# Seven products instead of eight for weight pair 3 in the output projection, with five raw slots and another planner table

## The chip, the cores and the metric

The kernel runs on one core of one Trainium2 chip. The metric is the device time of one execution, in microseconds (us). The core's engines each run their own instruction stream: TensorE (PE, with its weight loads shown apart as PEld), VectorE (DVE), ScalarE (ACT), GpSimd (POOL) and SyncE (SP). SP and POOL mainly start DMA transfers here. The order of the instructions on each engine is fixed when the kernel is built; at run time an instruction waits only for the semaphores that its inputs and buffers need.

## The reference

Two layers of a hybrid encoder over 256 tokens of width 4096, all in float32. Cut to what matters:

```python
for l in range(2):
    h = rmsnorm(x, norm_w[l])
    proj = h @ w_in[l]                       # (256, 4096) x (4096, 11264)
    aq, ak, av, ag, rq, rk, rv, rg = split(proj)
    a_out = silu(ag) * gqa_attention(rope(rmsnorm(aq)), rope(rmsnorm(ak)), av)
    r_out = silu(rg) * rmsnorm(bidirectional_retention(rope(rq), rope(rk), rv))
    x = x + concat(a_out, r_out) @ w_out[l]  # (256, 4096) x (4096, 4096)
return rmsnorm(x, final_norm)
```

Nearly all arithmetic is in the two projections, and they read 500 MB of weights once.

## The kernel before

**Three matmuls a product.** A float32 product is made of three matmuls in a faster format. A weight tile is split into a high part `whi` (a cast on ACT) and the rest `wlo` (a subtraction on DVE); the activations are split the same way into `x8h`, `x8l` (or `x7h`, `x7l`). PE does high times high and high times low (line 1683) and then low times high (line 1693).

**Blocks, pairs, pages.** The weights are worked off in 30 blocks of 1024 output columns: 11 of `w_in` and 4 of `w_out` in each layer. In a block the 4096 rows are taken as 16 pairs of 128-row tiles. With the two column halves and the two token halves a pair is a 2x2 by 2x2 block product: **eight** products, from two pages of 128x1024 weights, or **seven** by a Strassen-like scheme. `SEVENS` lists, for each of the four stages (w_in and w_out of layer 0, then of layer 1), the pairs that take seven: 2, 5, 8, 9, 11 and 13 everywhere. The products add up in PSUM banks M1 to M8, which `combine` folds into the two result pages `ca` and `cb` at a block's end, while PE is already in the next block.

**What a seven costs beside PE.** It needs sums of weight quarters. The first two quarters are loaded (`wraw`, 512 KB), copied by ACT to `wv`, and POOL starts a DMA that adds a second tensor from memory onto `wv` (line 729; `twice_in` or `twice_out`, 512 KB). DVE makes two more sums in `wu` from `wraw`, `wv` and the third quarter (`third`, 256 KB, line 552). So a seven gives four pages to split: `wraw` and `wv` and `wu` (128x1024 each) and `third` (128x512, parts `bhi` and `blo`). The activations of a seven need sums too: four in `xf` (128x128 each), then a split into `x7h`, `x7l`.

**Slots and the loads.** Raw pages land in `RAWS` = 6 slots, `wraw0` to `wraw5`. SP issues the load of the next page when a slot comes free (line 531): for an eight when DVE has made its `wlo`, for a seven when DVE has read it for `wu`. The loads follow the order of use, but the first page of a seven may be moved `A_EARLY` places forward in it:

```python
for i, g in enumerate(self.raws):
    if g.seven and i > RAWS + A_EARLY:
        self.raws.insert(i - A_EARLY, self.raws.pop(i))
```

With `A_EARLY` = 0 nothing is moved. High parts have a ring of five pages (`RING`), low parts of four.

**What sets the order.** A planner inside the kernel keeps a model of the time on PE, DVE and ACT while it writes the program, and puts the attention, the retention, the splitting of activations and the combining between the weight pages. The numbers in capitals (`RUSH`, `ADD_AHEAD`, `STEP_V`, `RELIEF`, ...) steer it; `PLANS` gives other values of some of them for single blocks (blocks 0 to 14 are layer 0, 15 to 29 layer 1). `SPREAD` to `SPREAD3` set where in the first block of each stage the sevens stand among the eights. In those four **opening blocks** the activations of the next stage have to be split while the last work of the stage before is still going on. All DVE and ACT instructions are recorded by one helper and so carry its line, 321.

## Time and profile before

| | us |
|---|---|
| median of 3 runs (2598.05 to 2601.19) | 2599.41 |
| the profiled execution | 2599.34 |
| its span, from the first to the last instruction | 2597.6 |

The profile is of one execution. A row of its page 5 gives a group of instructions: line, engine, operation, output and inputs, shape and count; then the busy time in us and the mean of one in ns; then how long the engine stood idle just before them and what ended that. The blocks lie one behind the other at some 83 us each; `w_out` of layer 0 opens at about 957 us, layer 1 at about 1290 us, and its `w_out` at about 2250 us.

### The profile page before, as it was taken

The numbers are of one execution on the slowest core, as the hardware profiler recorded it, in microseconds if no ns is written. First come the engines' busy times: TensorE is split into PE (matmuls) and PEld (weight loads), VectorE is DVE, ScalarE is ACT, GpSimd is POOL, SyncE is SP. The second block draws the span as 40 slices with busy tenths as digits, with TensorE's granted clock in tenths as the row PEclk, the third lists the DMA queues.
The fourth block names the chain that finished last, engine by engine and source line by source line (L and its number), as shares of the span: only waits on it lengthen the run. The fifth ranks groups of instructions, "written<-read, shape, count | busy, mean of one in ns | idle before, by whom it ended". The sixth has DMA issues, their size and how long they took to land.

```text
span 2597.6 us, 34368 instructions
## 1 busy us (share of the span) xinstructions
PE 2581.8 (99%) x11560; PEld 2135.2 (82%) x11560; DVE 2215.3 (85%) x2710; ACT 1853.6 (71%) x2626; POOL 398.6 (15%) x548
## 2 busy tenths in 40 slices
PE   9999999999999999999999999999999999999998
PEld 7888888888888888888878888888888888888886
DVE  7898888888789898777979888889888798987777
ACT  8877777766666788656887667776666667886655
POOL 0111221221102100211111112221201021000000
PEclk9999999999999999999999999999999999999999
DMA  9988988888778778988888879888887787788886
GB/s 314 305 237 277 289 242 254 281 247 263 221 220 260 230 235 227 271 269 248 275 253 261 250 239 279 246 270 268 259 257 222 208 259 242 220 229 251 250 243 194
DMA packets 206594, 653.52 MB, mean 252 GB/s; under 512 B 24784, under 2 KB 31440, under 8 KB 206416
## 3 DMA queue, kind: packets, MB, share of 16 engines
q1 hardware_dynamic: 147040, 472.99, 51.8%
q0 software_dynamic: 58656, 177.24, 30.7%
q8 instruction: 90, 1.47, 0.2%
q10 hardware_dynamic: 720, 1.10, 0.1%
q14 instruction: 88, 0.72, 0.1%
HBM read 607.19 MB, written 44.04 MB: 251 GB/s over the span
## 4 chain that ended last, share of the span: by engine, by line
PE 94%; DMA 2%; DVE 2%; ACT 1%; issue 1%; SPq 0%; DVEq 0%; POOLq 0%; POOL 0%; ACTq 0%
PE M L1683 60%; PE M L1693 30%; PE M L1158 1%; PE M L1157 1%; PE M L1156 1%; DMA ca<-in_x 1%; DVE wlo L321 1%; ACT whi L321 1%; DMA third<-in_w_out 0%; PE M L1677 0%; DMA wraw<-in_w_out 0%; DVE cb L321 0%; DMA whole<-in_w_in 0%; ACT ca L321 0%; DVE ca L321 0%
## 5 line engine op out<-in xcount | busy, mean ns | idle before, releaser
L321 DVE TENSOR_TENSOR wlo<-wraw,whi 128x1024 fp32r<-128x1024 f32 (+1 forms) x774 | 935.3, 1215 | 172.8 <-issue 61.2
L321 ACT CAST whi<-wraw 128x1024 fp32r<-128x1024 f32 (+1 forms) x776 | 800.1, 1045 | 297.1 <-PE M L1683 283.0
L1683 PE MATMUL M<-whi,x8h 128*128 128x512 f32 x2368 | 922.5, 390 | 1.0 <-DVE cb L321 0.8
L1683 PE MATMUL M<-whi,x8l 128*128 128x512 f32 x2368 | 921.8, 389 | 0.0
L1693 PE MATMUL M<-wlo,x8h 128*128 128x512 f32 x2364 | 676.3, 389 | 0.2 <-DVE wlo L321 0.2
L1683 PEld LDWEIGHTS M<-whi,x8h 128*128 128x128 f32 x2368 | 444.6, 188 | 94.9 <-DVE cb L321 1.5
L1683 PEld LDWEIGHTS M<-whi,x8l 128*128 128x128 f32 x2368 | 444.6, 188 | 92.4 <-DVE x8l L321 0.3
L1693 PEld LDWEIGHTS M<-wlo,x8h 128*128 128x128 f32 x2364 | 442.2, 188 | 91.4 <-DVE wlo L321 1.0
L1683 PE MATMUL M<-whi,x7h 128*128 128x512 f32 x1080 | 420.5, 389 | 0.2 <-ACT whi L321 0.2
L1683 PE MATMUL M<-whi,x7l 128*128 128x512 f32 x1080 | 420.3, 389 | 0.0
L1693 PE MATMUL M<-wlo,x7h 128*128 128x512 f32 x1080 | 334.4, 390 | 0.7 <-DVE wlo L321 0.6
L729 POOL DMA_DIRECT2D wv<-in_twice_in x132 | 118.5, 898 | 1068.6 <-ACT wv L321 923.8
L321 ACT CAST whi<-wu 128x1024 fp32r<-128x1024 f32 x180 | 189.3, 1052 | 91.9 <-DVE wu L321 54.2
L321 ACT CAST whi<-wv 128x1024 fp32r<-128x1024 f32 x180 | 189.0, 1050 | 91.5 <-PE M L1683 51.9
L321 DVE TENSOR_TENSOR wlo<-wv,whi 128x1024 fp32r<-128x1024 f32 x180 | 219.6, 1220 | 37.3 <-PE M L1693 30.7
L321 ACT COPY wv<-wraw 128x1024 f32<-128x1024 f32 x180 | 188.9, 1049 | 74.7 <-DMA wraw<-in_w_out 35.2
L321 DVE TENSOR_TENSOR wlo<-wu,whi 128x1024 fp32r<-128x1024 f32 x180 | 219.1, 1217 | 24.8 <-PE M L1693 16.7
L1693 PEld LDWEIGHTS M<-wlo,x7h 128*128 128x128 f32 x1080 | 202.4, 188 | 44.1 <-DVE wlo L321 2.5
L1683 PEld LDWEIGHTS M<-whi,x7h 128*128 128x128 f32 x1080 | 202.8, 188 | 42.6 <-ACT whi L321 0.9
L1683 PEld LDWEIGHTS M<-whi,x7l 128*128 128x128 f32 x1080 | 202.8, 188 | 41.8
L321 DVE TENSOR_TENSOR wu<-wu,third 128x512 f32<-128x512 f32 x180 | 124.6, 692 | 7.0 <-DMA third<-in_w_in 0.8
L321 DVE TENSOR_TENSOR wu<-wraw,wv 128x512 f32<-128x512 f32 x180 | 123.1, 684 | 8.7 <-DMA wv<-in_twice_in 6.3
(249 smaller groups left out, 2292.0 us busy)
## 6 DMA issues: line engine op xcount, KB each, us to landing
wraw<-in_w_in SPq DMA_DIRECT2D x568, 512.0 KB, 5.2
wraw<-in_w_out SPq DMA_DIRECT2D x208, 512.0 KB, 5.4
wv<-in_twice_in POOLq DMA_DIRECT2D x132, 512.0 KB, 7.5
third<-in_w_in SPq DMA_DIRECT2D x132, 256.0 KB, 5.8
wv<-in_twice_out POOLq DMA_DIRECT2D x48, 512.0 KB, 8.1
third<-in_w_out SPq DMA_DIRECT2D x48, 256.0 KB, 5.7
full<-next_dram POOLq DMA_DIRECT2D x18, 512.0 KB, 9.5
p_dram<-room POOLq DMA_DIRECT2D x64, 128.0 KB, 3.4
```

Source lines behind the costliest of these rows:

```text
L321: return call(out, *args, **kwargs)
L729: self.adds.pop(0)[1]()
L1156: nc.tensor.matmul(out, a[0], b[0], start=start, stop=False)
L1157: nc.tensor.matmul(out, a[0], b[1], start=False, stop=False)
L1158: nc.tensor.matmul(out, a[1], b[0], start=False, stop=stop)
L1683: nc.tensor.matmul(acc[name], a[i], g.hi[h], start=m == first[name] and not i, stop=False)
L1693: nc.tensor.matmul(acc[name], a, g.lo[h], start=False, stop=m == final[name])
```

## The change

Pair 3 takes seven products in stages 1 and 3, the eight `w_out` blocks; in `w_in` it stays an eight. `EVER`, the pairs that are a seven anywhere, grows from six to seven, and with it the `x7h` and `x7l` pages. The raw slots go from six to five, and `A_EARLY` from 0 to 1. The positions in the opening blocks and the planner's table are others, so nearly every row of every engine's order has another neighbour. Over the whole program PE has 11542 instructions in place of 11566: each of the eight blocks loses one product of three matmuls. DVE has 2752 in place of 2712, ACT 2436 in place of 2409; POOL gains eight DMA starts onto `wv`, and SP eight of `third` and eight fewer of `wraw`.

```diff
-RAWS = 6
-A_EARLY = 0
+RAWS = 5
+A_EARLY = 1
...
-RUSH = 1.0
+RUSH = 2.0
...
-ADD_AHEAD = 1.0
+ADD_AHEAD = 3.0
...
 PLANS = {
-    1: {'LOW_AHEAD': 5.0},
-    6: {'TIGHT_A': 8},
...
+    0: {'STEP_V': 3.0, 'BANK_REST': 0.5, 'LOW_AHEAD': 1.0, 'RELIEF': 1.0, 'AT_ONCE': 3},
+    1: {'STEP_V': 2.5, 'QUEUE': 1.0},
...
-SEVENS = ((2, 5, 8, 9, 11, 13), (2, 5, 8, 9, 11, 13), (2, 5, 8, 9, 11, 13), (2, 5, 8, 9, 11, 13))
+SEVENS = ((2, 5, 8, 9, 11, 13), (2, 3, 5, 8, 9, 11, 13), (2, 5, 8, 9, 11, 13), (2, 3, 5, 8, 9, 11, 13))
...
-SPREAD = (3, 5, 8, 11, 12, 13)
-SPREAD1 = (4, 7, 8, 10, 12, 14)
-SPREAD2 = (2, 3, 6, 7, 10, 13)
-SPREAD3 = (6, 7, 9, 11, 12, 14)
+SPREAD = (4, 5, 7, 11, 12, 13)
+SPREAD1 = (4, 6, 7, 10, 11, 12, 15)
+SPREAD2 = (2, 3, 6, 7, 12, 13)
+SPREAD3 = (3, 6, 7, 9, 11, 12, 13)
```

Three places in the order, all of layer 0. **Place A** is on DVE where the last `w_in` block ends and the first `w_out` block begins: the combining of the finished block (`cb`, `ca` from the banks M), and behind it the low part of the first weight page of `w_out` that is needed next (`wlo_8773` before, `wlo_8805` in the change; the numbers only tell buffers apart). Before:

```order
L321 TENSOR_TENSOR wlo_8727<-wraw1_8533,whi_8708 128x1024
L321 TENSOR_TENSOR x7l_8697<-xf_8698,x7h_8696 128x640
L321 TENSOR_TENSOR cb_8644<-ca_8643,M6_8244 128x512
L321 TENSOR_TENSOR ca_8643<-cb_8644,M7_8150 128x512
L321 SCALAR_TENSOR_TENSOR cb_8644<-ca_8643,M5_8147 128x512
L321 SCALAR_TENSOR_TENSOR cb_8644<-cb_8644,M5_8147 128x512
L321 TENSOR_TENSOR cb_8644<-cb_8644,out_8757 128x512
L321 TENSOR_TENSOR cb_8644<-cb_8644,M8_7952 128x512
L321 TENSOR_TENSOR wlo_8773<-wraw2_8591,whi_8722 128x1024
```

The same place on DVE in the change:

```order
L327 TENSOR_TENSOR wlo_8756<-wraw0_8616,whi_8732 128x1024
L327 TENSOR_TENSOR cb_8669<-ca_8668,M6_8249 128x512
L327 TENSOR_TENSOR ca_8668<-cb_8669,M7_8144 128x512
L327 SCALAR_TENSOR_TENSOR cb_8669<-ca_8668,M5_8139 128x512
L327 SCALAR_TENSOR_TENSOR cb_8669<-cb_8669,M5_8139 128x512
L327 TENSOR_TENSOR cb_8669<-cb_8669,out_8773 128x512
L327 TENSOR_TENSOR cb_8669<-cb_8669,out_8785 128x512
L327 TENSOR_TENSOR ca_8668<-ca_8668,M4_7967 128x512
L327 TENSOR_TENSOR ca_8668<-ca_8668,M2_7971 128x512
L327 TENSOR_TENSOR wlo_8805<-wraw3_8634,whi_8740 128x1024
```

The two sums onto `ca` now stand ahead of the low part, and the second sum onto `cb` reads a copy that ACT made (`out`) instead of bank M8; the `x7l` that stood here has moved up.

**Place B** is on ACT some 60 us earlier, in the last `w_in` block: sixteen small copies that move a result page (`ca<-room`, the last step of a retention pair), between the casts of weight pages (`whi`). Before:

```order
L321 ACTIVATE D_8094<-D_8094 128x1024
L321 COPY ca_7806<-room_8172 32x256 x4
L321 CAST whi_8185<-wraw4_8003 128x1024
L321 COPY ca_7806<-room_8172 32x256 x4
L321 CAST whi_8213<-wv_8050 128x1024
L321 CAST bhi_8215<-third_8048 128x512
L321 COPY wv_8230<-wraw1_8145 128x1024
L321 CAST whi_8238<-wraw5_8018 128x1024
L321 COPY ca_7806<-room_8172 32x256 x4
L321 CAST whi_8251<-wraw3_8076 128x1024
```

The same stretch on ACT in the change:

```order
L327 ACTIVATE D_8086<-D_8086 128x1024
L327 CAST whi_8173<-wraw0_8010 128x1024
L327 COPY ca_7800<-room_8163 32x256 x12
L327 CAST whi_8217<-wv_8042 128x1024
L327 CAST bhi_8219<-third_8040 128x512
L327 COPY wv_8232<-wraw1_8137 128x1024
L327 COPY ca_7800<-room_8163 32x256 x4
L327 CAST whi_8247<-wraw4_8068 128x1024
```

The cast that stood between the first two groups of copies is now ahead of them, and twelve copies follow each other with no cast among them.

**Place C** is on DVE about 45 us behind place A, in the first `w_out` block. The digit behind `wraw` is the slot. In the change `wraw2_9239` is loaded into slot 2 when `wlo_9237` has been made from the page before it there:

```order
L327 TENSOR_TENSOR wlo_9213<-wv_9052,whi_9184 128x1024
L327 TENSOR_TENSOR wlo_9237<-wraw2_9017,whi_9196 128x1024
L327 TENSOR_TENSOR blo_9202<-third_9064,bhi_9201 128x512
L327 TENSOR_TENSOR wlo_9245<-wraw1_9076,whi_9216 128x1024
L327 TENSOR_TENSOR wlo_9294<-wraw2_9239,whi_9285 128x1024
```

Only two rows stand between the one that frees slot 2 and the one that reads the page loaded into it. Before, the rows of the same place use three different slots, none of them twice:

```order
L321 TENSOR_TENSOR wlo_9233<-wraw5_8999,whi_9195 128x1024
L321 TENSOR_TENSOR wlo_9246<-wv_9056,whi_9217 128x1024
L321 TENSOR_TENSOR wlo_9256<-wraw3_9043,whi_9225 128x1024
L321 TENSOR_TENSOR blo_9231<-third_9054,bhi_9230 128x512
L321 TENSOR_TENSOR wlo_9287<-wu_9212,whi_9249 128x1024
L321 TENSOR_TENSOR wlo_9289<-wraw0_9084,whi_9261 128x1024
```

## The prediction

> **What bounds the kernel now.** I read the page first, then the chain in order of time, then the windows, then who waits for whom. The page's head, its chain and three groups:

> ```profile
> PE 2581.8 (99%) x11560; PEld 2135.2 (82%) x11560; DVE 2215.3 (85%) x2710; ACT 1853.6 (71%) x2626; POOL 398.6 (15%) x548
> PE 94%; DMA 2%; DVE 2%; ACT 1%; issue 1%; SPq 0%; DVEq 0%; POOLq 0%; POOL 0%; ACTq 0%
> L1683 PE MATMUL M<-whi,x8h 128*128 128x512 f32 x2368 | 922.5, 390 | 1.0 <-DVE cb L321 0.8
> L1693 PE MATMUL M<-wlo,x8h 128*128 128x512 f32 x2364 | 676.3, 389 | 0.2 <-DVE wlo L321 0.2
> L1683 PEld LDWEIGHTS M<-whi,x8h 128*128 128x128 f32 x2368 | 444.6, 188 | 94.9 <-DVE cb L321 1.5
> ```

> PE is busy 99% and makes 94% of the chain. Busy time is not pace, though: a matmul lasts 390 ns and overlaps the next. The pace comes from the chain in order of time, where each row is eight high matmuls and four low ones follow unlisted:

> ```profile
> 1763.87 1.81 PE M L1683 x8
> 1766.59 1.81 PE M L1683 x8
> ```

> From start to start are 2.72 us for twelve matmuls, **0.2267 us each**. Does PE ever fall out of this pace? The windows (length, then busy us and count of PE, PEld, DVE, ACT and POOL, the granted clock, the DMA share, GB/s):

> ```profile
> 924.00:1008.00 84.00, 84.00 (x389) 70.22 (x388) 79.48 (x118) 68.25 (x111) 6.93 (x9) 1.00 0.73 220
> 1092.00:1176.00 84.00, 84.00 (x373) 69.54 (x372) 65.44 (x68) 51.55 (x61) 13.34 (x18) 1.00 0.86 262
> 1176.00:1260.00 84.00, 84.00 (x372) 69.58 (x371) 66.08 (x78) 56.40 (x78) 16.07 (x23) 1.00 0.87 274
> 1260.00:1344.00 84.00, 83.25 (x360) 66.62 (x359) 74.88 (x105) 72.92 (x121) 10.03 (x12) 1.00 0.84 244
> 1344.00:1428.00 84.00, 83.20 (x366) 68.19 (x365) 73.96 (x101) 63.20 (x96) 13.39 (x16) 1.00 0.86 258
> ```

> 84 us hold 370.5 matmuls of 0.2267 us. The two middle `w_out` windows have them all (the shorter ones of attention and retention lift the counts, most in the first row); the two around the opening of layer 1 lack 15, so PE stood still there for 3.4 us. The weight loads' waits from 1280 to 1400 us say by whom:

> ```profile
> PEld M L1693 <- DVE wlo L321: 2.2, 5, 0.6
> PEld M L1683 <- DVE cb L321: 1.2, 1, 1.2
> PEld M L1683 <- DVE ca L321: 1.0, 2, 0.7
> PEld M L1683 <- ACT whi L321: 0.9, 2, 0.6
> PEld M L1683 <- DVE x8l L321: 0.3, 1, 0.3
> ```

> These are 5.6 us in eleven waits; a load runs one matmul ahead, so about 0.2 us of each is no loss to PE, and 3.4 us are left. Both ways agree. So PE sets the time nearly everywhere at a clock of 1.00, and DVE and ACT count only in the opening blocks, where DVE is busy 79 of 84 us.

> [...]

> **The change part by part.**

> *Products.* Eight blocks lose one product of three matmuls: 24 x 0.2267 = **5.4 us off PE**. Nothing hides it, PE being the chain.

> *What pair 3 adds beside PE, in each w_out block.* An eight has two casts and two low parts; a seven has three and a half of each, the copy to `wv` and two `wu` sums:

> ```profile
> L321 DVE TENSOR_TENSOR wlo<-wv,whi 128x1024 fp32r<-128x1024 f32 x180 | 219.6, 1220 | 37.3 <-PE M L1693 30.7
> L321 DVE TENSOR_TENSOR wu<-wu,third 128x512 f32<-128x512 f32 x180 | 124.6, 692 | 7.0 <-DMA third<-in_w_in 0.8
> L321 ACT CAST whi<-wv 128x1024 fp32r<-128x1024 f32 x180 | 189.0, 1050 | 91.5 <-PE M L1683 51.9
> L321 ACT CAST bhi<-third 128x512 fp32r<-128x512 f32 x180 | 111.2, 618 | 15.1 <-PE M L1683 14.5 <-DMA third<-in_w_in 0.4
> ```

> With about 0.69 us for each 128x512 operation on DVE and 0.62 us for the half cast, DVE gets 3 x 1.22 + 3 x 0.69 - 2 x 1.22 = 3.3 us more, ACT 4 x 1.05 + 0.6 - 2 x 1.05 = 2.7 us. By the middle windows DVE has 18 us free in a block and ACT 28 to 32, so this costs nothing there. Without that cover it would be 8 x 3.3 = 26 us. The transfers grow by 512 + 256 - 512 = 256 KB a block, 1 us at 262 GB/s, beside a DMA share of 0.86: also covered. The eight starts more on POOL stand on an engine busy 15%.

> *Five slots, and sevens' pages one place up.* This is the part that can bite. The loads, and what SP and ACT wait for:

> ```profile
> wraw<-in_w_in SPq DMA_DIRECT2D x568, 512.0 KB, 5.2
> wraw<-in_w_out SPq DMA_DIRECT2D x208, 512.0 KB, 5.4
> SPq L531 <- DVE wlo L321: 1343.6, 541, 7.9
> ACT wv L321 <- DMA wraw<-in_w_out: 35.2, 17, 6.4
> ACT wv L321 <- DMA wraw<-in_w_in: 32.9, 25, 3.8
> ACT whi L321 <- PE M L1683: 362.0, 393, 3.9
> ```

> SP always stands waiting for a slot, so a load starts when DVE frees one; 5.4 us later it has landed, and a cast of 1.05 us follows before DVE can use it: about 6.5 us, in which DVE needs other work. I summed DVE's rows in the order between the row that frees a slot and the row that reads the next page from it. Before, the smallest sum is 8.7 us, so no load makes DVE wait. In the change 24 of some 770 lie below 6.8 us (the same with 0.3 us for the issue) and lack **43 us together**, 1.8 us on average. Most stand in middle blocks. There ACT waits 393 times for PE to free a high page, so the split pages are as far ahead as their rings allow, and DVE's 18 free us take these waits. Two of the largest lie in `w_out` openings: place C (1.8 us of work, 5 us short) and one in layer 1 at about 2295 us (two low parts and a `blo`, 3.5 us of work, 3.3 us short). On the other side `A_EARLY` takes some of the 68 us in which ACT waited to copy a seven's first page.

> [...]

> *Opening of w_out in layer 0* (places A and B). DVE from 897 to 962 us of the trace: its window, its only waits, its low part and the matmul that uses it:

> ```profile
> 897.00:962.00 65.00, 65.00 (x294) 54.04 (x293) 60.65 (x83) 52.44 (x79) 5.17 (x8) 1.00 0.76 234
> DVE wlo L321 <- ACT whi L321: 3.9, 5, 1.5
> 958.74 1.22 DVE L321 TENSOR_TENSOR wlo<-wraw,whi 128x1024 fp32r<-128x1024 f32 x1
> 962.27 0.62 PE L1693 MATMUL M<-wlo,x8h 128*128 128x512 f32 x2
> ```

> The low part ends at 959.96 and is used at 962.27: 2.3 us in hand. In the change's order the same stretch of PE holds more on DVE: eight more `xf` sums, one more `x7l`, one more `D` product, `wTl`, and the two sums onto `ca` of place A. Their rows:

> ```profile
> L321 DVE TENSOR_TENSOR xf<-full 128x128 f32<-128x128 f32 x3 | 0.9, 285 | 0.0
> L321 DVE TENSOR_TENSOR x7l<-xf,x7h 128x640 fp32r<-128x640 f32 x3 | 2.5, 819 | 0.0
> L321 DVE SCALAR_TENSOR_TENSOR D<-M,D 128x512 f32<-128x512 f32 x1 | 0.7, 679 | 0.0
> L321 DVE TENSOR_TENSOR ca<-ca,M 128x512 f32<-128x512 f32 x2 | 1.3, 678 | 0.0
> ```

> 8 x 0.285 + 0.82 + 0.68 + 1.22 + 2 x 0.68 = 6.4 us, a little less back to back, say 6. Against them stand 2.3 us in hand and the 3.9 us of waits for ACT, if these go. If they all go, nothing is lost; if none go, 3.7 us. Place B has fewer casts behind copies at its start, but then twelve copies in a row, so I take half the waits as gone: 2 us short. Part of what was moved up (`wTl`, `ca`) no longer follows, so I set **+1.5 us**; with place C on top the bounds are 0 and +5.

> *Opening of layer 1.* The 3.4 us come from rows that lie otherwise now; the stage keeps six sevens. From 0 to 5.4 us can stand there afterwards; nothing in the profile says more, so I take half: **-1.7 us** (-3.4 to +2).

> *Opening of w_out in layer 1.* One set of `xf` sums more, and the load that is 3.3 us short: 0 to +3.3; **+1.0 us**.

> *The rest*, the other short loads and the first block: **+0.5 us**, bounds 0 and +10.7 (a quarter of the 43 us). The last block keeps its order of products, and the end behind the last matmul has the same instructions: 0.

> Sum: -5.4 + 1.5 - 1.7 + 1.0 + 0.5 = **-4.1 us**. The profiled execution took 2599.34 us (span 2597.6), the median of the runs is 2599.41; from either, **2595.2 us**, or -0.16%.

> **The rivals.**
> 1. *Nothing is given back*: the openings lose no more than before, or the planner's table also cures layer 1. 2590 to 2594.2. For it: the trace lost only 3.4 us in the middle although DVE had 2.3 us in hand at place A; against it: the forced waits of five slots.
> 2. *More is given back* in the openings, from no gain up to their upper bounds: -5.4 + 5 + 2 + 3.3 = +4.9 is the most, so 2599.3 to 2604.3.
> 3. *Slower: five slots.* Loads land later than 5.4 us, and DVE's waits reach PE in the middle blocks. The price is the part of the 43 us that isn't covered: at a quarter -5.4 + 10.7 = +5.3, 2604.6; at a half +16, 2615. It decides from the point where DVE is less than about 2 us ahead of PE when such a load is due. Against it: ACT and DVE run at the rings' limit in those blocks.
> [...]
> That the products aren't removed is no rival: the order has 24 matmuls fewer.

> **How the numbers follow.** Forecast (2594.2 to 2599.3) 0.42; rival 1, 0.40; rival 2, 0.06; rival 3, 0.09; rival 4, 0.03. A measurement of this kernel tells about 0.2%, 5.2 us, from no change, so faster begins below 2594.2 and slower above 2604.6: 0.40 faster, 0.51 same, 0.09 slower. Range 2590 to 2602: below it lies the case where all of layer 1's loss goes and nothing comes, above it rival 3.

> **What would show it.** Right: 24 matmuls fewer on PE at the same 0.2267 us; waits of PE on `wlo` or `whi` only at the four openings and the end, at 957 to 1045 us and 2245 to 2300 us where there were none; ACT waiting less for `wraw` at its copies and more for it at its casts; waits of DVE on ACT behind place C. Wrong: gaps of PE in middle `w_out` blocks, one each 83 us (rival 3), or no gap at all at places A and C (rival 1).

## The result, and the profile after

| | before | changed |
|---|---|---|
| median of 9 runs each (us) | 2599.27 (2598.05 to 2601.19) | 2606.68 (2603.23 to 2607.58) |
| the profiled execution | 2599.34 | 2607.58 |
| its span | 2597.6 | 2605.8 |

The ratio is 1.0027 with a 95% interval of 1.0018 to 1.0036: **slower by 7.4 us**, where 4.1 us less were predicted. The page of the changed kernel: its head, the first row of its chain, the group of high matmuls.

```profile
PE 2582.3 (99%) x11536; PEld 2132.2 (82%) x11536; DVE 2236.3 (86%) x2750; ACT 1869.3 (72%) x2653; POOL 403.3 (15%) x556
PE 85%; DVE 5%; issue 4%; DMA 4%; ACT 2%; POOL 0%; DVEq 0%; POOLq 0%; SPq 0%; ACTq 0%
L1689 PE MATMUL M<-whi,x8h 128*128 128x512 f32 x2128 | 830.1, 390 | 6.7 <-ACT whi L327 3.4
```

PE's share of the chain fell from 94 to 85%, and its idle time before this group rose from 1.0 to 6.7 us. The windows say where (columns as before; the last two rows are the opening of `w_out` in layer 1):

```profile
924.00:1008.00 84.00, 83.00 (x379) 68.60 (x378) 79.80 (x117) 72.42 (x119) 6.04 (x8) 1.00 0.71 220
1092.00:1176.00 84.00, 84.00 (x372) 69.55 (x371) 67.83 (x73) 55.78 (x66) 15.06 (x20) 1.00 0.88 267
1176.00:1260.00 84.00, 84.00 (x372) 69.57 (x371) 69.22 (x80) 58.48 (x79) 16.89 (x24) 1.00 0.88 267
1260.00:1344.00 84.00, 82.61 (x360) 66.66 (x359) 75.21 (x104) 68.77 (x110) 8.04 (x10) 1.00 0.86 258
1344.00:1428.00 84.00, 80.40 (x342) 65.59 (x341) 67.50 (x96) 61.28 (x103) 13.65 (x17) 0.96 0.80 231
2268.00:2352.00 84.00, 82.59 (x375) 68.23 (x374) 75.83 (x101) 69.36 (x107) 11.00 (x12) 1.00 0.78 220
2352.00:2436.00 84.00, 82.77 (x366) 68.21 (x365) 66.75 (x71) 53.64 (x63) 7.76 (x9) 1.00 0.85 251
```

The middle `w_out` windows hold 372 matmuls as before: pair 3's extra work costs nothing there, and no wait has come into them. The openings have lost matmuls, the window from 1344 us most, with 342 for 366; only the one from 1260 us holds as many as before. In layer 1's `w_out` the two windows held 380 and 372 before. The row from 1344 us also has a granted clock of 0.96, which no window of before shown above has. Finer windows of the changed kernel in it:

```profile
1370.00:1372.00 2.00, 0.21 (x1) 0.19 (x1) 2.00 (x3) 2.00 (x6) 0.00 (x0) 1.00 0.96 363
1372.00:1374.00 2.00, 1.15 (x3) 0.71 (x3) 2.00 (x5) 2.00 (x5) 0.00 (x0) 0.53 1.01 395
1374.00:1376.00 2.00, 2.00 (x6) 1.52 (x6) 1.55 (x3) 0.58 (x2) 0.00 (x0) 0.50 0.19 35
1376.00:1378.00 2.00, 2.00 (x6) 1.57 (x5) 0.00 (x0) 1.04 (x1) 0.00 (x0) 0.50 0.67 244
```

PE stands still while DVE and ACT are fully busy, and when it may go on, it goes on at half clock. Two of the nine executions, of 2603.2 and 2604.0 us, had a granted clock of 0.999 over all, the other seven, the profiled one among them, 0.997 or 0.998 at 2606.2 us and more. The loss therefore has two parts, the wait and the slow matmuls behind it, and counting both needs the distance from one matmul's start to the next. I summed it over every 512-wide matmul of the trace from 20 us on, less the pace of 0.2267 us, and over every 256-wide one less 0.1175 us:

| us that PE lost beyond its pace | `w_out` of layer 0 opens, 850 to 1100 | layer 1 opens, 1250 to 1400 | `w_out` of layer 1 opens, 2200 to 2450 | all the rest | sum |
|---|---|---|---|---|---|
| before | 0.3 | 4.1 | 0.4 | 4.5 | 9.3 |
| changed | 4.2 | 9.8 | 4.3 | 5.3 | 23.6 |
| difference | +3.9 | +5.7 | +3.9 | +0.8 | +14.3 |

14.3 - 5.4 us for the products is +8.9; the spans differ by 8.2, since the first 20 us and the end behind the last matmul, which the sum leaves out, are 0.7 us shorter.

Who lets PE wait most, over the whole span of the changed kernel (us in total, times, longest):

```profile
PE M L1689 <- ACT whi L327: 3.4, 3, 1.4
PE M L1689 <- ACT x8h L327: 2.7, 1, 2.7
PE M L1689 <- DVE x8l L327: 2.3, 3, 1.3
PE M L1699 <- DVE wlo L327: 1.5, 3, 0.9
```

The longest is the stop at 1369 us. Before it, in order of time and on several engines (start, duration, operation, and the idle time ahead of it with its releaser):

```profile
1317.25 1.06 ACT L327 COPY wv<-wraw 128x1024 f32<-128x1024 f32 x1 [2.60 <-DMA wraw<-in_w_in]
...
1351.96 2.00 ACT L327 COPY wv<-wraw 128x1024 f32<-128x1024 f32 x2
1353.31 1.80 POOL L735 DMA_DIRECT2D wv<-in_twice_in  x2 [6.68 <-ACT wv L327]
1361.78 0.69 DVE L327 TENSOR_TENSOR wu<-wraw,wv 128x512 f32<-128x512 f32 x1 [2.81 <-DMA wv<-in_twice_in]
1371.04 0.70 ACT L327 CAST x8h<-cb 128x256 fp32r<-128x256 f32 x2
1371.79 0.54 PE L1689 MATMUL M<-whi,x8h 128*128 128x512 f32 x1 [2.74 <-ACT x8h L327]
1373.19 0.79 PE L1689 MATMUL M<-whi,x8l 128*128 128x512 f32 x1 [0.85 <-DVE x8l L327]
```

A raw page lands late, the copies on ACT slip, POOL's adding DMA follows them, DVE waits 2.8 us for its sum, and the activations `x8h` and `x8l`, which stand behind it on both engines, come late to PE. ACT's waits for raw pages over the whole span:

```profile
ACT wv L327 <- DMA wraw<-in_w_in: 58.4, 32, 4.9
ACT wv L327 <- DMA wraw<-in_w_out: 41.0, 23, 4.4
ACT whi L327 <- DMA wraw<-in_w_in: 33.1, 26, 4.9
ACT whi L327 <- DMA wraw<-in_w_out: 11.9, 9, 2.5
```

144 us, where before had 68, all of it at copies.

### The profile page after: what moved, and what is told of

It is laid out like the page before. It is cut to its first block, busy times and chain, and to the rows that moved or that the text cites. A ratio compares the mean times of both kernels' runs of the same rounds, so it can differ in the third digit from the quotient of the medians.

```text
span 2605.8 us, 34445 instructions
## 1 busy us (share of the span) xinstructions
PE 2582.3 (99%) x11536; PEld 2132.2 (82%) x11536; DVE 2236.3 (86%) x2750; ACT 1869.3 (72%) x2653; POOL 403.3 (15%) x556
## 4 chain that ended last, share of the span: by engine, by line
PE 85%; DVE 5%; issue 4%; DMA 4%; ACT 2%; POOL 0%; DVEq 0%; POOLq 0%; SPq 0%; ACTq 0%
PE M L1689 54%; PE M L1699 27%; DVE wlo L327 2%; DMA wv<-in_twice_out 2%; DMA wraw<-in_w_out 1%; PE M L1162 1%; PE M L1164 1%; PE M L1163 1%; ACT whi L327 1%; PE M L1683 1%; DVE cb L327 1%; ACT ca L327 0%; DVE ca L327 0%; DMA wraw<-in_w_in 0%; DVE x7l L327 0%
## 5 line engine op out<-in xcount | busy, mean ns | idle before, releaser
L327 DVE TENSOR_TENSOR wlo<-wraw,whi 128x1024 fp32r<-128x1024 f32 x766 | 925.8, 1215 | 176.5 <-ACT whi L327 85.3
L327 ACT CAST whi<-wraw 128x1024 fp32r<-128x1024 f32 (+1 forms) x768 | 790.4, 1045 | 276.9 <-PE M L1689 216.1
L1689 PE MATMUL M<-whi,x8h 128*128 128x512 f32 x2128 | 830.1, 390 | 6.7 <-ACT whi L327 3.4
L1689 PE MATMUL M<-whi,x8l 128*128 128x512 f32 x2128 | 829.9, 390 | 2.3 <-DVE x8l L327 2.3
L1699 PE MATMUL M<-wlo,x8h 128*128 128x512 f32 x2124 | 612.2, 390 | 1.6 <-DVE wlo L327 1.5
L1689 PE MATMUL M<-whi,x7h 128*128 128x512 f32 x1304 | 508.1, 390 | 0.1
L1689 PE MATMUL M<-whi,x7l 128*128 128x512 f32 x1304 | 507.5, 389 | 0.0
L1689 PEld LDWEIGHTS M<-whi,x8h 128*128 128x128 f32 x2128 | 400.3, 188 | 92.0 <-ACT whi L327 4.6
L1689 PEld LDWEIGHTS M<-whi,x8l 128*128 128x128 f32 x2128 | 400.3, 188 | 86.3 <-DVE x8l L327 3.7
L1699 PEld LDWEIGHTS M<-wlo,x8h 128*128 128x128 f32 x2124 | 397.8, 188 | 85.3 <-DVE wlo L327 3.7
L1699 PE MATMUL M<-wlo,x7h 128*128 128x512 f32 x1304 | 396.3, 389 | 0.2
L327 ACT COPY wv<-wraw 128x1024 f32<-128x1024 f32 x188 | 197.0, 1050 | 105.9 <-DMA wraw<-in_w_in 58.4
L327 ACT CAST whi<-wv 128x1024 fp32r<-128x1024 f32 x188 | 197.3, 1050 | 98.9 <-PE M L1689 47.6
## 6 DMA issues: line engine op xcount, KB each, us to landing
wraw<-in_w_in SPq DMA_DIRECT2D x568, 512.0 KB, 5.3
wraw<-in_w_out SPq DMA_DIRECT2D x200, 512.0 KB, 5.7
wv<-in_twice_in POOLq DMA_DIRECT2D x132, 512.0 KB, 7.6
wv<-in_twice_out POOLq DMA_DIRECT2D x56, 512.0 KB, 8.2
full<-next_dram POOLq DMA_DIRECT2D x18, 512.0 KB, 10.8
```

The source lines that it names most:

```text
L327: return call(out, *args, **kwargs)
L1689: nc.tensor.matmul(acc[name], a[i], g.hi[h], start=m == first[name] and not i, stop=False)
L1699: nc.tensor.matmul(acc[name], a, g.lo[h], start=False, stop=m == final[name])
```

## The experiments

Two theories stood against each other. **Slots**: the fifth slot comes free too late at the openings. **Order**: the new order of rows puts too much ahead of PE's inputs there, whatever the slots. Ratios are to the kernel before, run beside each experiment.

**A sixth slot under the changed order.** Room for it comes from memory that leaves the order alone: the rotary tables share one tile, and the decay's distances are read from another one, so positions and decays come out otherwise here. `A_EARLY` stays 1.

```diff
-            self.slots = [f"wraw{_i}" for _i in range(RAWS)]
+            self.slots = [f"wraw{_i}" for _i in range(RAWS + 1)]
...
-    while weights.slots:
+    while len(weights.slots) > 1:
```

> The changed kernel with its order of instructions kept row by row on all five engines, and a sixth raw slot in SBUF: each page goes to the slot that has been free longest, so a load waits for the release before the one it waits for in the change. To make room, the sine table is written over the cosine table and the distances are read from the gains, so positions and decays come out otherwise; the instructions and their shapes stay. Theory S (five slots: pages land just in time, and a late one finds DVE and ACT without reserve, which PE meets at the next opening): 2597 to 2601 us, with the PE stalls of the change at 966, 1368, 2330 and 2362 us gone or under half. Theory O (the order of the openings itself, whatever the number of slots): 2604 to 2607 us, the same stalls of 1 to 4 us at the same places.

2596.31 us, ratio 0.9991 (0.9982 to 1.0000): 2.1 us below before, span 2594.7. Its two windows at layer 1, and ACT's waits for raw pages over its span:

```profile
1260.00:1344.00 84.00, 84.00 (x372) 69.55 (x371) 78.33 (x109) 72.69 (x117) 9.18 (x11) 1.00 0.87 266
1344.00:1428.00 84.00, 82.84 (x365) 68.00 (x364) 71.69 (x99) 62.78 (x101) 13.87 (x17) 1.00 0.81 244
```

```profile
ACT wv L327 <- DMA wraw<-in_w_in: 11.0, 8, 3.1
ACT whi L327 <- DMA wraw<-in_w_in: 6.0, 6, 1.8
ACT wv L327 <- DMA wraw<-in_w_out: 3.7, 1, 3.7
ACT whi L327 <- DMA wraw<-in_w_out: 3.6, 3, 1.3
```

Every row stands where it stood (some read or write another tile), the waits fall from 144 to 24 us, and the same two copies and the sum behind them come 4.6 and 6.2 us earlier:

```profile
1347.37 2.00 ACT L327 COPY wv<-wraw 128x1024 f32<-128x1024 f32 x2
1355.54 0.69 DVE L327 TENSOR_TENSOR wu<-wraw,wv 128x512 f32<-128x512 f32 x1 [1.14 <-DMA wv<-in_twice_in]
```

So the slots cost about 10 us. With six of them the rest of the change gains some 2 us, at the edge of what can be told from nothing. Not every stop went: the one at 966 us stayed.

**Five slots without the rest of the change**, on the kernel before:

```diff
-RAWS = 6
-A_EARLY = 0
+RAWS = 5
+A_EARLY = 1
```

> The kernel before with RAWS 5 and A_EARLY 1 alone: no product removed, the table of before. The planner knows of the five slots and lays the order out for them. Theory S: slower, 2608 to 2625 us, with new stalls of PE in first blocks, openings and the last blocks. Theory O: 2598 to 2602 us, since five slots by themselves cost nothing and no opening was laid out anew on purpose.

2611.67 us, 1.0052 (1.0038 to 1.0066): 13.3 us slower than before. PE loses 13.1 us more in the sum of the table above, 8.4 of them ahead of 850 us and 3.9 where layer 1 opens. The most is one stop in the program's first block: two matmuls at 64 us start 4.6 us apart, and 13 at half clock follow. The planner laid out another order for five slots here, and `A_EARLY` is 1 as well, so this isn't the price of the slot alone; but without the products, too, five slots made the kernel slower, and at other places.

**The changed kernel with the planner's table of before.**

```diff
-RUSH = 2.0
+RUSH = 1.0
...
-ADD_AHEAD = 3.0
+ADD_AHEAD = 1.0
...
-    0: {'STEP_V': 3.0, 'BANK_REST': 0.5, 'LOW_AHEAD': 1.0, 'RELIEF': 1.0, 'AT_ONCE': 3},
+    1: {'LOW_AHEAD': 5.0},
...
```

> The changed kernel with the planner's table, RUSH and ADD_AHEAD of before: products, five slots and the loads one place up stay. Theory S: the slots' cost stays and what the new table saved goes, 2608 to 2625 us. Theory O (the new table's openings are what costs): 2600 us or less, with the stalls at 909, 966 and 1368 us gone.

2619.52 us, 1.0081 (1.0067 to 1.0095). The new table saves about 13 us with five slots. It isn't what makes the change slower; without it PE loses 35.4 us.

**Stops of PE of several lengths.** On the kernel before, two matmuls with a tile of zeros stand ahead of the low matmul of the sixty-first product in eleven blocks. POOL writes the tile 4 to 32 times between them, and the second waits for it; both add zero.

```diff
+PAUSES = {4: 4, 5: 6, 6: 8, 7: 10, 8: 12, 17: 14, 18: 16, 19: 20, 20: 24, 21: 28, 22: 32}
...
+                for _ in range(2 if m == 60 and count[0] - 1 in PAUSES else 0):
+                    nc.tensor.matmul(acc[name], zero, g.lo[h], start=False, stop=False)
+                    for _ in range(PAUSES[count[0] - 1]):
+                        nc.gpsimd.memset(f32(zero), 0.0)
```

> The kernel before with one pause of PE in the middle of each of eleven blocks (blocks 4 to 8 and 17 to 22, counted from 0): PE reads a tile of zeros, POOL then fills that tile again 4, 6, 8, 10, 12, 14, 16, 20, 24, 28 and 32 times, and PE's next matmul waits for it. Two matmuls with zeros are added at each. The length of each pause is read from the trace. Theory C (an idle PE loses its clock): pauses under 3 us cost their own length and the next matmuls keep 0.227 us; pauses over 4.5 us are followed by 7 to 16 matmuls of 0.427 us at a granted clock of 0.50, 1.4 to 3.2 us more each; between them it depends on when they begin. Theory D (the slow matmuls at 1373 us in the change come from what is special at that opening): no slow matmuls behind any pause, whatever its length.

2674.74 us in a single run. Its windows around the shortest stop and around a longer one:

```profile
391.00:393.00 2.00, 1.12 (x5) 0.58 (x4) 2.00 (x3) 1.98 (x3) 0.64 (x4) 1.00 0.76 257
393.00:395.00 2.00, 1.77 (x8) 1.47 (x9) 0.79 (x2) 1.31 (x2) 0.99 (x5) 1.00 0.43 140
...
576.00:579.00 3.00, 0.84 (x4) 0.38 (x2) 1.85 (x3) 3.00 (x5) 1.64 (x8) 0.97 0.96 297
579.00:582.00 3.00, 3.00 (x7) 2.42 (x8) 1.26 (x2) 1.31 (x2) 1.65 (x8) 0.50 0.09 33
```

Behind a distance of 1.5 us between two matmuls the clock stays at 1.00; behind 2.55 us seven matmuls come at 0.427 us each, twice the pace, and that adds 1.6 us. Distances from 2.55 to 8.85 us brought 7 to 13 such matmuls, 1.5 to 2.9 us. So theory C is right that an idle PE loses its clock, and wrong that stops under 3 us are free of it. Its limits were an estimate that fits the runs at hand: under the table of before no matmul was slow behind 2.83 us, with five slots 13 were behind 4.6 us, and the 6.83 us at half clock of the change hold 16 at 0.427 us each. In this run a stop of some 3 us cost about half as much again; the last section has one that did not.

**The sixth slot only around the openings, and only elsewhere.** `OPENINGS` holds the three blocks around each of the three openings; the slot is given out when the loads reach such a block and withdrawn behind it. The second kernel has `not in`. Both make room as the first experiment did.

```diff
+OPENINGS = (10, 11, 12, 14, 15, 16, 25, 26, 27)
+def SIXTH(block):
+    return block in OPENINGS
...
+                if SIXTH(g.block) and not self.sixth:
+                    self.sixth = True
+                    self.slots.insert(0, "wraw5")
```

> As the run with a sixth slot and the order of the change (the same leavings: sine over cosine, distances from the gains), but the sixth slot takes pages only while pages of blocks 10 to 12, 14 to 16 and 25 to 27 are loaded, the blocks at the openings of w_out and of layer 1. Theory at the place (a late page costs where PE stands, so the slot helps in the openings): 2597 to 2600 us, most of the 10 us between five and six slots. Theory reserve (the blocks ahead decide how far ACT and DVE are ahead when an opening comes): less than half of the 10 us, 2602 to 2606 us.

> The complement: the sixth slot takes pages in all blocks but 10 to 12, 14 to 16 and 25 to 27, so the openings have five. Same order, same leavings. Theory at the place: 2603 to 2607 us, the stalls at 966, 1368, 2330 and 2362 us as in the change. Theory reserve: 2597 to 2601 us, those stalls under half.

At the openings: 2596.93 us, 0.9994 (0.9985 to 1.0003). Elsewhere: 2607.47 us, 1.0033 (1.0021 to 1.0045). ACT's waits for raw pages, first of the kernel with the slot at the openings, then of the other:

```profile
ACT wv L334 <- DMA wraw<-in_w_in: 53.2, 34, 4.0
ACT whi L334 <- DMA wraw<-in_w_in: 33.7, 26, 4.5
ACT wv L334 <- DMA wraw<-in_w_out: 19.1, 10, 4.4
ACT whi L334 <- DMA wraw<-in_w_out: 10.8, 7, 2.5
```

```profile
ACT wv L334 <- DMA wraw<-in_w_in: 17.6, 11, 2.9
ACT wv L334 <- DMA wraw<-in_w_out: 17.0, 11, 3.7
ACT whi L334 <- DMA wraw<-in_w_in: 12.4, 10, 2.2
ACT whi L334 <- DMA wraw<-in_w_out: 10.3, 7, 2.5
```

The kernel that waits 117 us is the fast one, the one that waits 57 us is as slow as the change. How much ACT waits for raw pages doesn't decide; **where** it does, decides. In this order of rows the whole price of the missing slot lies at the openings.

**Each opening by itself.** The same kernel with another tuple:

```diff
-OPENINGS = (10, 11, 12, 14, 15, 16, 25, 26, 27)
+OPENINGS = (14, 15, 16)
```

```diff
-OPENINGS = (10, 11, 12, 14, 15, 16, 25, 26, 27)
+OPENINGS = (10, 11, 12, 25, 26, 27)
```

> As the run with the sixth slot in the blocks at the openings, but only while pages of blocks 14 to 16 are loaded, the opening of layer 1. By the stalls of the change (0.9 at 1297, 1.6 at 1334 to 1337, 2.9 and 1.2 at 1369 to 1372 and 3.2 of slow matmuls behind them, of which 1.5 to 1.7 stayed with six slots): 7 to 9 us less than the change, 2597.5 to 2600 us. Rival, that a late page anywhere weighs alike (three blocks of thirty, a tenth of the 10 us): 2604 us or more.

> The sixth slot only while pages of blocks 10 to 12 and 25 to 27 are loaded, the two openings of w_out. By the stalls of the change there (1.65 at 909 of which 0.5 stay, 0.6 at 2260, 0.35 at 2280, 1.6 at 2330, 1.5 at 2362): 4 to 5 us less than the change, 2601.5 to 2603.5 us; the slow matmuls at 1373 us stay. Rival (all of the price lies in layer 1's opening): 2605 us or more.

Layer 1 alone: 2602.21 us, 1.0015 (1.0006 to 1.0023), above what was expected. The two `w_out` openings alone: 2602.74 us, 1.0017 (1.0008 to 1.0026), as expected. Against the kernel before these are +3.3 and +3.9 us, the change is +7.4, and both together (the experiment above) -1.7. So the slot at layer 1's opening takes 4.1 us off, at the two `w_out` openings 3.5, at all three 9.1. The parts make 7.6; each of these differences is known to some 2 us either way, so the 1.5 us between 7.6 and 9.1 can't be told from noise. In the sum by stretches the slot given only to layer 1 still leaves 4.0 us lost where layer 1 opens (1.6 with the `w_out` slots as well), and the slot given only to `w_out` takes the loss where layer 1 opens from 9.8 to 6.1. A stage may begin with what reserve the one before left; these are single traces, and no run shows it apart.

**A version that computes everything and has the sixth slot.** The rotary tables move into one of the thirteen pages, whose ring has the room at that time:

```diff
-        c = t(sp, [P, MT, HD], "C")
-        s = t(sp, [P, MT, HD], "S")
+        if kind == "ak":
+            lodging[0] = sp.tile([P, 4, SEQ], F32, tag="pg", name="CS", bufs=PAGES)
+        c, s = (lodging[0][:, i].rearrange("p (m d) -> p m d", m=MT) for i in ((0, 1) if kind == "ak" else (2, 3)))
...
-            self.slots = [f"wraw{_i}" for _i in range(RAWS)]
+            self.slots = [f"wraw{_i}" for _i in range(RAWS + 1)]
```

> A version that computes everything: the order of the change, and a sixth raw slot in memory that is freed by putting the two rotary tables of a layer into one of the thirteen pages, which the planner doesn't count. Theory S: 2595 to 2600 us, below the kernel before by 0 to 3 us, since 24 products are gone (5.4 us) and about 3 us of stalls of the order itself remain (966, 1031 and 1367 us with six slots); a page more in use may cost up to 2 us around 180 to 230 us, where pages are scarce. Theory O: 2604 us or more.

2597.08 us, 0.9994 (0.9985 to 1.0003): clearly below the change, and not to be told from before. It agrees with the first experiment within 0.8 us, so the memory freed there is not what made that one fast.

## Why the prediction was wrong

The sign was wrong, and the time lies outside the range. Term by term, from the sum by stretches (the sixth slot's column is the first experiment):

| term | predicted | changed | changed order, six slots |
|---|---|---|---|
| products | -5.4 | -5.4 | -5.4 |
| opening of `w_out`, layer 0 | +1.5 (0 to +5) | +3.9 | +3.2 |
| opening of layer 1 | -1.7 (-3.4 to +2) | +5.7 | -2.3 |
| opening of `w_out`, layer 1 | +1.0 (0 to +3.3) | +3.9 | +0.1 |
| the rest | +0.5 (0 to +10.7) | +0.8 | +2.0 |
| sum | -4.1 | +8.9 | -2.4 |

**Products: right.** The pace is the same. With 24 matmuls fewer, before's span of 2597.6 - 5.4 and the difference in lost time, 12.3 - 9.3, give 2595.2 for the six-slot kernel; its span is 2594.7. The weight loads' share is 82% although the full windows leave PE no free place (372 x 0.2267 us make 84.3 us in windows of 84), so PE is the bound here; no run shows what rival 4 had its 0.03 for, a PE that is not the bound and 2599.3 us.

**Pair 3's work in the middle: right.** Full windows, as shown. Its transfers are covered with six slots, but not quite with five. The changed kernel's page has the `third` of `w_out` (count, KB each, median us from issue to landing), and its waits of ACT from 2340 to 2364 us say what such a load does:

```profile
third<-in_w_out SPq DMA_DIRECT2D x56, 256.0 KB, 7.4
```

```profile
ACT bhi L327 <- DMA third<-in_w_out: 5.1, 1, 5.1
...
ACT wv L327 <- DMA wraw<-in_w_out: 3.5, 1, 3.5
```

The median was 5.7 us before, and is 5.2 in the last experiment's page, with six slots and the same transfers. ACT stands 5.1 us for a `third`, then 3.5 us for the next raw page, and PE loses 1.5 us at 2362 us.

**Five slots: the step that failed.** The prediction gave every load one landing time, 5.4 us, got 24 short loads of 43 us, and found most in middle blocks where they are covered. It so left the slots 0.5 us in the rest and a share of the two `w_out` terms, and nothing at layer 1's opening. They cost 11.3 us of PE's time (23.6 - 12.3): 8.0 at layer 1's opening, 4.5 at the two of `w_out`, while elsewhere the changed kernel lost 1.2 less. The prediction's own rows held a sign: ACT waited 42 times for a raw page, up to 6.4 us, where by the one landing time no load was late for DVE. Landings spread: before, half of the `wraw` loads take up to 5.3 us, one in ten over 8.6, one in twenty over 9.2. With 8.7 us, a cast of 1.05 and 0.35 for the issue, 10.1 us must lie between the row that frees a slot and the row that reads the next page. By the same sums of DVE's rows, 12 of 770 loads lack that before, 5 us in all; in the change 146 of 763 lack 276 us, 33 loads and 81 us of it in the three stretches of the table above, little more than their share of the time. In before the median sum is 15.3 us, in the change 13.0: a slot fewer takes reserve from the loads everywhere. That the slow landings are what PE felt is worked out here, not shown load by load; ACT's waits for raw pages, 144 us for 68, agree with it.

**Opening of layer 1: the term that it broke.** It said that nothing in the profile tells more and took half the loss as gone. The profile could have told where late pages would be felt: here PE already waited on DVE's rows, and DVE was busy 74 to 75 of 84 us. The predicted value would have been good with six slots (-2.3); five cost 8.0 us more, about 2.6 of them by 13 matmuls at half clock (13 x 0.2) in the profiled execution, which the prediction had no price for.

**The `w_out` openings: right mechanism, too small.** In layer 0 the order does cost: of the +3.9 us, 3.2 stay with six slots. Some 1.7 us are lost behind place A, from 955 to 990 us, and there the sixth slot changes nothing. Behind place B, from 900 to 930 us, 1.7 us become 0.7 with six slots, and 0.5 to 0.9 us stand at 1020 to 1060 us, at neither place. PE's waits from 950 to 968 us, of the changed kernel, and then with six slots:

```profile
PE M L1699 <- DVE wlo L327: 0.9, 1, 0.9
```

```profile
PE M L1700 <- DVE wlo L327: 1.0, 1, 1.0
```

Place C was to be 5 us short. DVE did wait there, 2.8 us at 1010 us, but PE nowhere. In layer 1 the +3.9 are the slots, since six leave +0.1.

**The waits of ACT.** "More at its casts" was right (0 to 45 us), "less at its copies" wrong (68 to 99): putting a seven's page one place up didn't make good the slot taken away.

**The rivals.** Rival 3 had the cause, and its lowest time of 2604.6 lies near the 2606.7 measured, but it looked for the waits in middle blocks and got a chance of 0.09 for that reason. One slot more was the remedy (2596.31 us), while the sign named for this rival, gaps in middle blocks, one each 83 us, did not show: the gaps stand at three openings only.

**Open**: how much of an opening's loss comes from the stage before it, and why `third` lands later without the slot at the `w_out` openings (6.9 to 7.4 us, for 5.1 to 5.5 with it), while five slots in the order of before left it at 5.8.

## What to carry to other kernels

Size a ring of buffers by the slow landings (here one in ten over 8.6 us), not by the median one (5.3 us), and look first at the stage where the engines that feed the bound have no time to spare; here the middle of a stage hid what its opening didn't. Whether a buffer or an order costs the time is told by one kernel that changes the count and leaves every row where it is. And read a wait by its place: 117 us of them cost nothing here, and 57 us cost ten.

## What the hardware showed that was not expected

```profile
1367.52 0.61 PE L1715 MATMUL M<-wlo,x7h 128*128 128x512 f32 x2
1369.10 0.51 PE L1705 MATMUL M<-whi,x8h 128*128 128x512 f32 x1 [0.96 <-ACT x8h L334]
1370.48 0.50 PE L1705 MATMUL M<-whi,x8l 128*128 128x512 f32 x1 [0.88 <-DVE x8l L334]
...
1371.44 0.63 PE L1705 MATMUL M<-whi,x8h 128*128 128x512 f32 x1
1371.87 0.63 PE L1705 MATMUL M<-whi,x8l 128*128 128x512 f32 x1
```

The starts are 1.36 and 1.38 us apart, and two matmuls later seven come at half clock, the first two of them shown. At the same place 1.13 and 1.35 us bring seven in the last experiment, 1.13 and 0.92 us none in the first, and neither does any single distance up to 1.8 us (1.77 us at 909 us in the changed kernel). Nor did 2.83 us, in the changed kernel with the table of before, where the matmuls behind the stop keep their pace at a clock of 1.00:

```profile
1240.79 0.50 PE L1683 MATMUL M<-whi,x8h 128*128 128x512 f32 x1 [2.44 <-ACT whi L321]
```

So the length alone doesn't decide. In the clock record of the changed kernel's trace the half clock lasts 6.83 us, from 1372.11 to 1378.94 us, and the granted clock changes at 400, 402 and 759 times 3.413 us behind its first rise; in that of before it changes once, at 757 times, behind the last matmul. In such steps, with each matmul counted at its pace, PE was busy for 0.12 of the one behind which the clock fell to half in the changed kernel, and for 0.52 or more of every other step at full clock of these two traces, from 20 us to the step ahead of the last matmul's. Of its two steps at half clock the first, 0.67 busy, did not bring the full clock back, the second, 1.00 busy, did. The 2.55 us fell into one step, 0.37 busy; the 2.83 us were cut by a border into two, 0.65 and 0.53 busy. What these stops cost beyond their length so went with where they fell among the steps, too.
